# Values of the last head group computed as features by tokens, its eight units mixed two to a bank, and the first two tiles of the output projection taken half by half

## The chip, the cores and the metric

The kernel runs on one NeuronCore of one Trainium2 chip. The metric is the device time of one execution in microseconds (us), as a median over runs. The names of the engines are those of the profile: PE is TensorE, DVE is VectorE, ACT is ScalarE, POOL is GpSimd, SP is the engine that issues most of the transfers. PE has two clock levels, 1.2 and 2.4 GHz; the profile gives the granted one as a share of the higher.

## The reference

A decoder trunk of two layers over 1,024 tokens of width 1,024, all in float32. Cut to what matters here, one layer is:

```python
hn = rmsnorm(h, norm1[i])
z = hn @ w_in[i]                       # 256 pool columns, then q, k, v of 768 columns each
u = z[..., :POOL_WIDTH]
q, k, v = jnp.split(z[..., POOL_WIDTH:], 3, axis=-1)
...                                    # partial rotary on q and k; 12 heads of 64
pool_out = pool_mixer(u, pool_w[i], pool_scale[i])
attn_out = dilated_mixer(q, k, v)      # 3 head groups ("patterns") of 4 heads, each with its own
                                       # window and dilation; weighted by their softmax denominators
h = h + jnp.concatenate([pool_out, attn_out], axis=-1) @ w_out[i]
hn = rmsnorm(h, norm2[i])
h = h + jnp.square(jax.nn.relu(hn @ w_up[i])) @ w_down[i]
gate = jax.nn.sigmoid(rmsnorm(h, norm3[i]) @ w_gate[i])
h = h + gate * (p[i] @ w_ple[i])
```

The change lies at the end of the input projection (the 256 v columns of the third pattern), in that pattern's product of probabilities and values, and in the first two of eight column tiles of `w_out`.

## The kernel before, in words

Activations lie transposed: a tile holds 128 features by 1,024 tokens. Each is kept as a pair of fp32r tiles, high part and low part (`h`, `l`), and so is each weight (`wh`, `wl`), so that one product is three matmuls per 128 rows of the contraction: `wh` by `h`, `wh` by `l`, `wl` by `h`. `products` issues the 8 x 3 matmuls of 512 columns for one weight tile of 128 columns and one half (512) of the tokens.

The input projection goes in this order: q, k, v of pattern 0, of pattern 1, q and k of pattern 2, the two pool tiles `u0` and `u1`, and last v of pattern 2. The attention of a pattern is eight units of 128 queries. A unit takes four steps: `scores` on PE, `softmax` on DVE and ACT, `turn` (PE transposes of the probabilities into a bank tagged "e", and a copy to `et`), and `mix` (PE products of `et` with the values into a bank tagged "o", evacuated by `out`). These steps are strewn between the matmuls of the projection.

What decides that order is a clock in the program that builds the kernel, `Clock`. Every matmul of a product moves it on by an estimate (`tick`), and work that was put down for later (`at`, `go` with a delay, a `yield` in a generator) is issued when the clock passes its time. `need` and `until` are different: if something is not yet issued, they move the clock to the next pending piece of work and issue it, again and again, until it is, without a matmul in between. The order so found is fixed on each engine's queue; on the chip an instruction that waits holds up all that stands behind it on its engine.

The weights come through `Weights.next`: it needs the asked tile's high and low parts issued (`ck.need`), and starts the tile after it (`begin`), one of eight row blocks every 900 ns of that clock.

In the stage that is changed the other engines have this to do:

- the pool mixer: `mix_sums(1)` on POOL builds window sums `pa`, `pb` of `u1`; `mix_out` on DVE makes `py` from them; two matmuls `pm` on PE (one for each half) into "e" banks, evacuated to `cat0` and `cat1` by ACT (high part) and DVE (low part)
- `joint`: the weights of the three patterns, by small DVE operations, one PE transpose `jt` into an "e" bank, the DVE copy `jw`, and transfers through DRAM (`wt_d`) into tiles `wb` that are broadcast over the partitions
- `weigh`: DVE multiplies a pattern's output `o` by `wb`, ACT and DVE split it into the pair `cat2` to `cat7`, which the output projection reads.

There are 8 PSUM banks: three tagged "mm", two "s", two "e" and one "o". An "e" bank is given on when the copies out of it are done. The core of the code that is replaced, with `v2` as tokens by features:

```python
        for t in range(8):
            p = bank(f"v2p{L}", "mm", (128, 256))
            ...
                nc.tensor.matmul(p, h[:, tc_], wh, start=kk == 0, stop=False)
```

There the activations are the stationary operand and the weights the moving one, 256 columns, so no transpose of v is needed. Each unit's `mix` follows by itself once its 128 tokens are there.

Of the kernel before, what the change touches and what calls it, by code (L numbers as in the profile page):

```python
# [9 lines left out]
F32 = mybir.dt.float32  # L10
# [107 lines left out]
def body(nc, tc, pools, A, out):  # L118
# [3 lines left out]
    def blk(name, dt=F32, shape=(128, 1024)):  # L122
        return sb.tile(list(shape), dt, name=name, tag="b")

    def bank(name, tag, shape=(128, 512)):
        return ps.tile(list(shape), F32, name=name, tag=tag)
# [4 lines left out]
    def hs(hf):  # L131
        return slice(hf * 512, hf * 512 + 512)
# [207 lines left out]
    for L in range(DEPTH):  # L340
        wi, wo, wu, wd, wg = (A[n][L] for n in ("w_in", "w_out", "w_up", "w_down", "w_gate"))
        g1 = G_N1 + 8 * L

        def col(part, g):
            return POOLW + 768 * part + 256 * g

        for g in range(NPAT):
            for part in range(2 if g == 2 else 3):
                for m in range(2):
                    groups.append([(wi, 0, 8, col(part, g) + 128 * m, 128, g1)])  # L350
        for m in range(2):
            groups.append([(wi, 0, 8, 128 * m, 128, g1)])
        groups.append([(wi, 4 * a, 4, col(2, 2), 256, g1) for a in range(2)])
        for m in range(8):
            groups.append([(wo, 0, 8, 128 * m, 128, None)])
        sevens.append(([(wu, 0, 4, 256 * j) for j in range(FF // 256)],
                       [(wd, a, n, 256 * t) for t, a, n in STEPS]))
        dn0.append(len(groups))
        for rep in range(2 if L == DEPTH - 1 else 1):
            for m in range(8):  # L360
                groups.append([(wg, 0, 8, m * 128, 128, None)])
            for m in range(2):
                pgroups.append([(A["w_ple"][L], 0, 2, m * 512, 512, None)])
# [177 lines left out]
    def pair(name):  # L541
        return blk(name + "H", F32R), blk(name + "L", F32R)

    def products(p, w, rhs, cols, first=True, last=True):
        n = len(w)
        ns = 0.42 * (cols.stop - cols.start)
        for i in range(n):
            (wh, wl), (h, l) = w[i], rhs[i]
            ck.need((id(h), cols.start // 512))
            nc.tensor.matmul(p, wh, h[:, cols], start=first and i == 0, stop=False)  # L550
            ck.tick(ns)
            nc.tensor.matmul(p, wh, l[:, cols], start=False, stop=False)  # L552
            ck.tick(ns)
            nc.tensor.matmul(p, wl, h[:, cols], start=False, stop=last and i == n - 1)  # L554
            if i + 1 < n:
                ck.tick(ns)
        ck.now += ns
# [65 lines left out]
    def layer(L, hT, norm, tabs):  # L623
# [96 lines left out]
        oT = {}  # L720
        vdone = set()

        def vok(g, n, p):
            return ((2, n) if g == 2 else (g, p, n // 4)) in vdone

        def in_v(g):
            vs = []
# [127 lines left out]
        def attend(g, q, k, vget, base, gap, late):  # L855

            o = [blk(f"o{g}{p}_{L}") for p in range(2)]
            oT[g] = o
            units = [Unit(g, n, q, k, vget, o) for n in range(8)]

            def alone(u):
                yield 1500.0
                while not vok(g, u.n, 0):
                    yield 500.0
                u.mix()

            def beats():
                t = ck.now
                for i in range(8 + 2 * late):
                    if 0 <= i - late < 8:  # L870
                        u = units[i - late]
                        u.turn()
                        if g == 2:
                            ck.go(alone(u))
                    if g < 2 and i >= 2 * late:
                        u = units[i - 2 * late]
                        while not (vok(g, u.n, 0) and vok(g, u.n, 1)):
                            yield 500.0
                        u.mix()
                    if i < 8:  # L880
                        units[i].scores()
                    t += gap
                    yield max(100.0, t - ck.now)
            ck.go(beats(), delay=base)

        for g in range(2):
            q = in_qk(f"q{g}", g)
# [3 lines left out]
                   5000.0, 5900.0, 1)  # L891
        q = in_qk("q2", 2)
        k = in_qk("k2", 2)
        v2 = [blk(f"v2{a}_{L}", F32, (128, 4, 256)) for a in range(2)]
        attend(2, q, k, lambda n, h: v2[n // 4][:, n % 4, 64 * h:64 * h + 64],
               3500.0, 2500.0, 2)


        us = [blk(f"u{m}_{L}") for m in range(2)]
# [118 lines left out]
        def weigh(g, p, hf):  # L1018
            i = 2 * g + p
            keys = {("wb", g, p)}  # L1020
            for n in range(4 * hf, 4 * hf + 4) if g == 2 else range(8):
                keys.add(("o", g, n, 1))
            while keys & ck.waiting:
                yield 300.0
            o = oT[g][p][:, hs(hf)]
            nc.vector.tensor_tensor(o, o, wbc[g, p][:, hs(hf)], op=OP.mult)
            used.append((g, p))
            if used.count((g, p)) == 2:
                del wbc[g, p]
            yield 800.0  # L1030
            yield from split(cat[2 + i], o, hf)
# [11 lines left out]
        for i in range(4):  # L1043
            cat[2 + i] = pair(f"cat{2 + i}_{L}")
            for hf in range(2):
                ck.go(weigh(i // 2, i % 2, hf), (id(cat[2 + i][0]), hf), W_0 + W_1 * (2 * i + hf))
        for t in range(8):
            p = bank(f"v2p{L}", "mm", (128, 256))
            tc_ = slice(t * 128, t * 128 + 128)
            for kk in range(8):  # L1050
                h, l = hT[kk]
                wh, wl = (x[:, kk % 4] for x in w[kk // 4])
                nc.tensor.matmul(p, h[:, tc_], wh, start=kk == 0, stop=False)
                nc.tensor.matmul(p, l[:, tc_], wh, start=False, stop=False)
                nc.tensor.matmul(p, h[:, tc_], wl, start=False, stop=kk == 7)
                if kk < 7:
                    ck.tick(330.0)
            nc.scalar.activation(v2[t // 4][:, t % 4], p, AF.Copy, scale=norm.rt[:, t:t + 1])
            ck.at(600.0, lambda t=t: vdone.add((2, t)))
            ck.tick(330.0)  # L1060
            if t in (3, 7):
                for i in (4, 5):
                    if t == 3:
                        cat[2 + i] = pair(f"cat{2 + i}_{L}")
                    hf = t // 7
                    ck.go(weigh(2, i % 2, hf), (id(cat[2 + i][0]), hf), 2500.0 + 900.0 * (i - 4))


        norm2 = Norm(f"b{L}")
# [95 lines left out]
        S7 = Seven(sevens[L][0], seq, f"u{L}", side=4)  # L1165

        catl = [cat[i] for i in range(8)]
        for m in range(6):
            w = W.next()
            if m == 5:  # L1170
                W.begin(W.i + 1, delay=5000.0)
            for hf in range(2):
                p = bank(f"po{L}", "mm")
                products(p, wk(w, range(8)), catl, hs(hf))
                ck.go(out_evac(p, m, hf))
# [413 lines left out]
```

## Time and profile before

| | |
|---|---|
| median of 3 runs | 2268.42 us (2268.37 to 2268.53) |
| the profiled execution, device time | 2269.02 us |
| its span from first to last instruction | 2267.2 us |
| PE busy | 2240.3 us (99%), 11088 matmuls |
| DVE busy | 1643.2 us (72%) |
| ACT busy | 1011.6 us (45%) |
| POOL busy | 313.9 us (14%) |
| granted PE clock, mean | 0.999 |
| chain that ended last | PE 91%, DVE 5%, DMA 1%, ACT 1%, POOL 1% |

A matmul's time in the profile runs from its start to its modelled end, and neighbours overlap; what a matmul costs is read from the distance between starts. In the chain the overlap is taken off already.

### The profile page before, as it was taken

How to read it: one execution, taken by the hardware profiler on the slowest of the kernel's cores; microseconds unless marked ns; L12 is line 12 of the kernel's file. 1: busy time of each engine (PE TensorE's matmuls, PEld its weight loads, DVE VectorE, ACT ScalarE, POOL GpSimd, SP SyncE). 2: the span in 40 equal slices, each digit the busy share in tenths (PEclk: the TensorE clock that was granted, in tenths of full speed). 3: DMA queues.
4: the chain of work that ended last, by engine and by line, in shares of the span. 5: the costliest groups of instructions: out<-in, count | busy, mean ns of one | idle time of the engine just before them, and what ended most of it. 6: DMA issues, size and time to landing. Idle time of an engine off the chain costs nothing.

```text
span 2267.2 us, 30544 instructions
## 1 busy us (share of the span) xinstructions
PE 2240.3 (99%) x11088; PEld 1849.0 (82%) x11088; DVE 1643.2 (72%) x3046; ACT 1011.6 (45%) x2147; POOL 313.9 (14%) x282
## 2 busy tenths in 40 slices
PE   8999999999999999999999999999999999999998
PEld 6887788888887888878887878888888878888888
DVE  6565757877778888796565567687777798888845
ACT  6244533533335434364324355444333453434645
POOL 5121135100000000022121122330000000000322
PEclk9999999999999999999999999999999999999999
DMA  6011133354448745431220122234445675546224
GB/s 186 19 48 20 39 94 112 124 167 150 150 143 271 239 135 171 149 112 47 61 62 19 39 49 61 81 112 153 153 154 160 209 247 175 162 140 181 69 62 134
DMA packets 296367, 275.63 MB, mean 122 GB/s; under 512 B 12476, under 2 KB 224056, under 8 KB 296216
## 3 DMA queue, kind: packets, MB, share of 16 engines
q1 hardware_dynamic: 293624, 270.04, 38.6%
q0 software_dynamic: 2272, 3.61, 0.9%
q8 instruction: 87, 1.43, 0.3%
q14 instruction: 64, 0.52, 0.1%
q10 hardware_dynamic: 320, 0.03, 0.0%
HBM read 200.99 MB, written 72.58 MB: 121 GB/s over the span
## 4 chain that ended last, share of the span: by engine, by line
PE 91%; DVE 5%; DMA 1%; ACT 1%; issue 1%; POOL 1%; SPq 0%; DVEq 0%; ACTq 0%
PE X L567 29%; PE Z L567 14%; PE Y L567 7%; PE in L552 5%; PE in L554 5%; PE in L550 5%; PE gt L554 3%; PE gt L552 3%; PE gt L550 3%; PE po L552 2%; PE po L550 2%; PE po L578 2%; PE po L554 2%; PE o L836 2%; PE s L785 2%
## 5 line engine op out<-in xcount | busy, mean ns | idle before, releaser
L458 POOL TENSOR_TENSOR sq_c<-sq_c,sqt_c 128x512 f32<-128x512 f32 x28 | 41.8, 1496 | 1162.0 <-ACT sqt_c L456 1161.1
L567 PE MATMUL X<-wP,d0p 128*128 128x512 f32 x768 | 180.2, 390 | 3.2 <-DVE acc L1294 2.5
L567 PE MATMUL X<-wP,d1p 128*128 128x512 f32 x768 | 180.1, 390 | 3.2 <-DVE acc L1294 2.5
L567 PE MATMUL X<-xP,u1p 128*128 128x512 f32 x768 | 182.2, 389 | 0.0
L567 PE MATMUL X<-xP,u0p 128*128 128x512 f32 x768 | 182.2, 389 | 0.0
L567 PEld LDWEIGHTS X<-wP,d0p 128*128 128x128 f32 x768 | 143.8, 188 | 34.6 <-ACT wP L1275 2.0
L567 PEld LDWEIGHTS X<-wP,d1p 128*128 128x128 f32 x768 | 143.8, 188 | 34.6 <-ACT wP L1275 2.0
L1277 DVE TENSOR_TENSOR wP<-wP 128x512 fp32r<-128x512 f32 x252 | 171.0, 697 | 0.9 <-ACT wP L1275 0.9
L567 PEld LDWEIGHTS X<-xP,u1p 128*128 128x128 f32 x768 | 143.9, 188 | 29.8
L567 PEld LDWEIGHTS X<-xP,u0p 128*128 128x128 f32 x768 | 143.9, 188 | 29.8
L1235 ACT ACTIVATE y<-y 128x1024 f32<-128x1024 f32 x64 | 67.3, 1055 | 199.2 <-DVE y L1232 199.1
L191 DVE SCALAR_TENSOR_TENSOR wl<-wr,gt,wh 128x128 fp32r<-128x128 f32 (+1 forms) x288 | 117.8, 440 | 44.4 <-ACT wh L197 44.1
L1275 ACT ACTIVATE wP<-wP 128x512 fp32r<-128x512 f32 x252 | 146.7, 617 | 0.2
L1294 DVE TENSOR_TENSOR acc<-acc,X 128x512 f32<-128x512 f32 x128 | 87.4, 683 | 55.6 <-PE X L567 55.6
L804 ACT ACTIVATE sm<-sm,nm 128x128 f32<-128x128 f32 (+1 forms) x192 | 84.3, 440 | 79.9 <-DVE nm L801 77.6
L197 ACT ACTIVATE wh<-wr,gt 128x128 fp32r<-128x128 f32 (+1 forms) x304 | 101.8, 397 | 0.9 <-DMA wr<-in_w_in_dram 0.8
L680 POOL TENSOR_TENSOR rot<-rot,s 128x512 f32<-128x512 f32 x48 | 61.6, 1288 | 255.6 <-DVE rot L678 136.7
L567 PE MATMUL Z<-wP,d1p 128*128 128x512 f32 x384 | 92.1, 389 | 1.0 <-DVE acc L1294 1.0
L567 PE MATMUL Z<-wP,d0p 128*128 128x512 f32 x384 | 92.1, 389 | 1.0 <-DVE acc L1294 1.0
L567 PE MATMUL Z<-xP,u1p 128*128 128x512 f32 x384 | 91.6, 389 | 0.0
L567 PE MATMUL Z<-xP,u0p 128*128 128x512 f32 x384 | 91.6, 389 | 0.0
L567 PEld LDWEIGHTS Z<-wP,d0p 128*128 128x128 f32 x384 | 72.0, 188 | 16.4 <-DVE acc L1294 1.4
(474 smaller groups left out, 5510.1 us busy)
## 6 DMA issues: line engine op xcount, KB each, us to landing
wP<-x_d SPq DMA_DIRECT2D x252, 256.0 KB, 3.4
x_d<-ys SPq DMA_DIRECT2D x64, 512.0 KB, 3.7
wr<-in_w_in_dram SPq DMA_DIRECT2D x40, 512.0 KB, 4.2
u0r<-in_w_up_dram SPq DMA_DIRECT2D x32, 512.0 KB, 5.1
x_d<-y SPq DMA_DIRECT2D x32, 512.0 KB, 2.8
u1r<-in_w_up_dram SPq DMA_DIRECT2D x32, 512.0 KB, 5.4
d0r<-in_w_down_dram SPq DMA_DIRECT2D x28, 512.0 KB, 6.2
d1r<-in_w_down_dram SPq DMA_DIRECT2D x28, 512.0 KB, 5.9
```

What stands on the lines that cost most here:

```text
L191: nc.vector.scalar_tensor_tensor(l[:, k], raw[:, k], gs[k], f(h[:, k]), op0=OP.mult, op1=OP.subtract)
L197: nc.scalar.activation(h[:, k], raw[:, k], AF.Copy, scale=gs[k])
L550: nc.tensor.matmul(p, wh, h[:, cols], start=first and i == 0, stop=False)
L552: nc.tensor.matmul(p, wh, l[:, cols], start=False, stop=False)
L554: nc.tensor.matmul(p, wl, h[:, cols], start=False, stop=last and i == n - 1)
L567: nc.tensor.matmul(p, w[:, a, i], x[:, b], start=first and i == 0 and a == b == 0, stop=i == n - 1 and a == 1, skip_group_check=not first)
L680: nc.gpsimd.tensor_tensor(a, a, tb["s"][:, hs(hf)], op=OP.mult)
L804: nc.scalar.activation(self.sm[:, p, hh], self.sm[:, p, hh], AF.Exp, bias=nm[:, h:h + 1], scale=0.125, accum_out=ml[g][:, n, 4 + h:5 + h])
L1235: nc.scalar.activation(y, y, AF.Square)
L1275: nc.scalar.activation(t[:, 0], f(t[:, 1]), AF.Copy)
L1277: nc.vector.tensor_tensor(t[:, 1], f(t[:, 1]), f(t[:, 0]), op=OP.subtract)
L1294: nc.vector.tensor_tensor(a, a, p, op=OP.add)
```

## The change

The version before computes v of pattern 2 as tokens by features with 192 matmuls of 256 columns. The version after computes it like every other v, as features by tokens, with 96 matmuls of 512 columns from two weight tiles that are both held (`ws`), half by half: both tiles for tokens 0 to 511, then both for 512 to 1023. Four DVE evacuations with the norm's scale go to `vts`. For each half `mix_half` transposes the two tiles on PE (eight transposes, through "e" banks), copies them on ACT to `v2`, and then issues the four units of the half together, two to a bank, one bank tagged "o" and one "s", with four ACT copies of 256 columns. The first two tiles of the output projection are also both taken before their products, and done as tile 0 and tile 1 for the first half, then for the second.

```diff
-        groups.append([(wi, 4 * a, 4, col(2, 2), 256, g1) for a in range(2)])
+        for m in range(2):
+            groups.append([(wi, 0, 8, col(2, 2) + 128 * m, 128, g1)])
...
-            def alone(u):
-                yield 1500.0
-                while not vok(g, u.n, 0):
-                    yield 500.0
-                u.mix()
...
-                        if g == 2:
-                            ck.go(alone(u))
...
-        for t in range(8):
-            p = bank(f"v2p{L}", "mm", (128, 256))
...
+        ws = [w, W.next()]
+        vts = []
+        for m in range(2):
+            vts.append(blk(f"vt2{m}_{L}"))
+            v2.append(blk(f"v2{m}_{L}", F32, (128, 8, 128)))
+
+        def mix_half(b):
+
+            yield 2200.0
+            for m in range(2):
+                p = bank(f"vp2_{L}", "e", (128, 4, 128))
+                for i in range(4):
+                    n = 4 * b + i
+                    nc.tensor.transpose(p[:, i], vts[m][:, n * 128:n * 128 + 128], ident)
+                ck.now += 430.0
+                nc.scalar.activation(v2[m][:, 4 * b:4 * b + 4], p, AF.Copy)
+            yield 2000.0
+            for c in range(2):
+                us_ = units2[4 * b + 2 * c:4 * b + 2 * c + 2]
+                op = bank(f"o2_{L}", "os"[c], (128, 2, 2, 128))
...
+        for hf in range(2):
+            for m in range(2):
+                p = bank(f"in{L}", "mm")
+                products(p, wk(ws[m], range(8)), hT, hs(hf))
+                nc.vector.tensor_tensor(vts[m][:, hs(hf)], p, norm.bc[:, hs(hf)], op=OP.mult)
+            ck.go(mix_half(hf))
...
-        for m in range(6):
+        w = W.next()
+        ws = [w, W.next()]
+        for hf in range(2):
+            for m in range(2):
+                p = bank(f"po{L}", "mm")
+                products(p, wk(ws[m], range(8)), catl, hs(hf))
+                ck.go(out_evac(p, m, hf))
+        ws = None
+        for m in range(2, 6):
```

The second `W.next()` of the v stage stands directly behind the first. At that point the second tile's eight row blocks are not issued yet, so `need` moves the builder's clock on until they are, and other work that was put down for that time is issued too. Three places show it; `_0` in a name is the layer, the last number tells buffers apart.

On PE, where the second pool tile's last product (`in_2646`, or `in_2640`) ends and the v stage begins. Before:

```order
L554 MATMUL in_2646<-h_7H,wl_2338 128x512
L1053 MATMUL v2p_2750<-wh_2501,h_0H 128x256
L1054 MATMUL v2p_2750<-wh_2501,h_0L 128x256
L1055 MATMUL v2p_2750<-wl_2502,h_0H 128x256
L944 MATMUL pm_2754<-py_2636,pw_135 128x512
L1053 MATMUL v2p_2750<-wh_2501,h_1H 128x256
```

After:

```order
L555 MATMUL in_2640<-h_7H,wl_2334 128x512
L938 MATMUL pm_2744<-py_2630,pw_135 128x512
L938 MATMUL pm_2751<-py_2630,pw_135 128x512
L976 MATMUL jt_2765<-cst,jt 96x128
L551 MATMUL in_2781<-h_0H,wh_2497 128x512
L553 MATMUL in_2781<-h_0L,wh_2497 128x512
```

Both `pm` of the first pool tile and the transpose `jt` now stand ahead of the stage; before, the second `pm` stood after 18 and `jt` after 42 of its 192 matmuls.

On PE, around the second pool tile's two `pm`. Before, they stand in the sixth and seventh of eight token tiles:

```order
L1055 MATMUL v2p_2953<-wl_2504,h_6H 128x256
L944 MATMUL pm_2993<-py_2892,pw_135 128x512
L1053 MATMUL v2p_2953<-wh_2503,h_7H 128x256
...
L836 MATMUL o_3015<-et_2625,v_0_2327 64x128 x4
L944 MATMUL pm_3022<-py_2892,pw_135 128x512
L1053 MATMUL v2p_3004<-wh_2501,h_3H 128x256
```

After (`in_2872` is the third of the four v products, `vp` are the banks of the first half's transposes, `vt` the evacuated tiles):

```order
L555 MATMUL in_2872<-h_0H,wl_2498 128x512
L938 MATMUL pm_2878<-py_2813,pw_135 128x512
L551 MATMUL in_2872<-h_1H,wh_2497 128x512
L553 MATMUL in_2872<-h_1L,wh_2497 128x512
L555 MATMUL in_2872<-h_1H,wl_2498 128x512
L551 MATMUL in_2872<-h_2H,wh_2497 128x512
L1054 MATMUL vp_0_2890<-cst,vt_0_2777 128x128 x4
L1054 MATMUL vp_0_2896<-cst,vt_0_2779 128x128 x4
L938 MATMUL pm_2905<-py_2813,pw_135 128x512
L553 MATMUL in_2872<-h_2L,wh_2497 128x512
```

The first of them now stands 51 matmuls of 512 columns into the stage, and the second seven places behind, after the transposes. In this version `vp_0_2896` and then `pm_2905` get the "e" bank of `vp_0_2890`, one after the other, each after ACT's copy out of it.

On DVE, between the evacuation of `u1` and that of the first half's second v tile (`vt_0_2779`), after the change:

```order
L988 TENSOR_TENSOR u_0_2329<-in_2640,rs_a_484 128x512
L191 SCALAR_TENSOR_TENSOR wl_2735<-wr_2495,gt,wh_2734 128x128
L539 SCALAR_TENSOR_TENSOR cat_0L<-pm_2744,gt,cat_0H 128x512
L191 SCALAR_TENSOR_TENSOR wl_2735<-wr_2495,gt,wh_2734 128x128 x2
...
L181 TENSOR_TENSOR wl_2776<-wr_2732,wh_2775 128x1024
L925 SCALAR_TENSOR_TENSOR py_2813<-pa_2717,cst,u_0_2329 64x1024
...
L535 TENSOR_TENSOR cat_0L<-o_0_879,cat_0H 128x512
L1077 TENSOR_TENSOR vt_0_2779<-in_2820,rs_a_484 128x512
L1020 TENSOR_TENSOR o_0_1703<-o_0_1703,wb 128x512 x2
L535 TENSOR_TENSOR cat_0L<-o_0_1703,cat_0H 128x512 x2
```

New behind `u` are the eight `wl` of the second v tile (before, a tile of 256 columns was all made ahead of `u`), and the two `vt` evacuations stand behind `py` and behind four multiplications and four splits of `weigh`. ACT's copy out of `vp_0_2890` stands behind both splits of `o_0_1703` and behind that of `pm_2878`.

## Rows read from the trace of the kernel before

**Rows 1.** Waits of PE over the span: total us, times, longest.

```profile
PE o L836 <- ACT v L1058: 0.6, 2, 0.3
```

**Rows 2.** Windows of the changed stage in layer 0 and layer 1.

```profile
281.46:313.87 32.41, 32.13 (x259) 28.01 (x258) 22.79 (x42) 14.26 (x35) 11.88 (x11) 1.00 0.46 116
1393.40:1425.80 32.40, 32.12 (x259) 28.00 (x258) 22.72 (x42) 14.23 (x35) 11.89 (x11) 1.00 0.46 116
```

**Rows 3.** Timeline of PE, layer 0: start us, us, instruction.

```profile
282.78 0.28 PE L1054 MATMUL v2p<-wh,h_1L 128*128 128x256 f32 x1
...
284.34 0.28 PE L1055 MATMUL v2p<-wl,h_5H 128*128 128x256 f32 x1
...
313.71 0.40 PE L550 MATMUL po<-cat_0H,wh 128*128 128x512 f32 x1
```

**Rows 4.** The chain that ended last: start us, us, what; overlap taken off.

```profile
248.99 1.07 PE o L836 x16
...
257.97 0.44 PE e L817 x4
...
281.97 0.86 PE pm L944 x2
...
286.90 0.59 PE o L836 x8
287.49 0.32 PE v2p L1053
...
380.00 21.76 PE po L578 x96
```

**Rows 5.** Timeline of DVE in the stage, layer 0.

```profile
282.89 0.68 DVE L994 TENSOR_TENSOR u<-in,rs_a 128x512 f32<-128x512 f32 x1
283.49 1.21 DVE L181 TENSOR_TENSOR wl<-wr,wh 128x1024 fp32r<-128x1024 f32 x1
...
289.26 0.29 DVE L985 COPY jw<-jt 96x128 f32<-96x128 f32 x1 [1.20 <-PE jt L982]
292.70 3.00 DVE L931 SCALAR_TENSOR_TENSOR py<-pa,cst,u 64x1024 f32<-64x1024 f32 x1 [3.16 <-POOL pa L911]
...
296.01 1.28 DVE L931 SCALAR_TENSOR_TENSOR py<-pb,cst,u 64x1024 f32<-64x1024 f32 x1
...
297.62 2.54 DVE L1026 TENSOR_TENSOR o<-o,wb 128x512 f32<-128x512 f32 x4
```

**Rows 6.** Timeline of POOL in the stage, layer 0.

```profile
283.65 3.01 POOL L905 TENSOR_TENSOR pa<-u 128x896 f32<-128x896 f32 x1 [34.03 <-DVE u L994]
...
287.29 1.84 POOL L905 TENSOR_TENSOR pb<-pa 128x768 f32<-128x768 f32 x1
...
292.48 0.19 POOL L911 COPY pa<-pb 128x4 f32<-128x4 f32 x1
292.75 1.88 POOL L910 TENSOR_TENSOR pb<-pa 64x1016 f32<-64x1016 f32 x1
294.57 1.20 POOL L911 COPY pb<-pa 64x8 f32<-64x8 f32 x1
```

**Rows 7.** Instructions of line L191: ns min/median/max, first and last start.

```profile
L191 DVE SCALAR_TENSOR_TENSOR wl<-wr,gt,wh x288: 334/345/1264, 30.6 to 1391.6; 128x128 fp32r<-128x128 f32 x136, 128x256 fp32r<-128x256 f32 x8
```

**Rows 8.** Timeline of ACT in the stage, layer 0.

```profile
279.29 0.57 ACT L827 ACTIVATE et<-e 128x512 f32<-128x512 f32 x1
...
306.56 0.68 ACT L536 ACTIVATE cat_0H<-pm,gt 128x512 fp32r<-128x512 f32 x1
...
309.06 0.62 ACT L532 ACTIVATE cat_0H<-o 128x512 fp32r<-128x512 f32 x1
```

**Rows 9.** Timeline of PE at the kernel's start, and a window behind its last matmul.

```profile
7.49 3.03 PE L605 MATMUL xp<-cst,x 128*128 128x128 f32 x13 [0.72 <-DMA x<-in_x_dram]
...
12.82 0.60 PE L605 MATMUL xp<-cst,x 128*128 128x128 f32 x4
...
2262.00:2264.00 2.00, 0.00 (x0) 0.00 (x0) 0.70 (x2) 0.61 (x1) 0.00 (x0) 0.50 0.57 214
```

More of the change, by code (lines that the diff above doesn't have):

```diff
@@ L723, in vok @@
         def vok(g, n, p):
-            return ((2, n) if g == 2 else (g, p, n // 4)) in vdone
+            return (g, p, n // 4) in vdone
         def in_v(g):
@@ L884, in attend @@
             ck.go(beats(), delay=base)
+            return units
         for g in range(2):
@@ L893, in layer @@
         k = in_qk("k2", 2)
-        v2 = [blk(f"v2{a}_{L}", F32, (128, 4, 256)) for a in range(2)]
-        attend(2, q, k, lambda n, h: v2[n // 4][:, n % 4, 64 * h:64 * h + 64],
-               3500.0, 2500.0, 2)
+        v2 = []
+        units2 = attend(2, q, k, lambda n, h: v2[h // 2][:, n, 64 * (h % 2):64 * (h % 2) + 64],
+                        3500.0, 2500.0, 2)
         us = [blk(f"u{m}_{L}") for m in range(2)]
@@ L1046, in layer @@
                 ck.go(weigh(i // 2, i % 2, hf), (id(cat[2 + i][0]), hf), W_0 + W_1 * (2 * i + hf))
-        for t in range(8):
-            p = bank(f"v2p{L}", "mm", (128, 256))
[L1049 to L1066, printed above, removed]
+        ws = [w, W.next()]
@@ new lines, in layer @@
+        vts = []
[15 more added lines that the diff above has]
+                op = bank(f"o2_{L}", "os"[c], (128, 2, 2, 128))
+                for i, u in enumerate(us_):
+                    for p, hh, h in u.heads:
+                        nc.tensor.matmul(op[64 * hh:64 * hh + 64, i, p], u.vget(u.n, h), u.et[:, p, hh, 0],
+                                         start=True, stop=True)
+                ck.now += 860.0
+                n = us_[0].n
+                for p in range(2):
+                    nc.scalar.activation(oT[2][p][:, n * 128:n * 128 + 256]
+                                         .rearrange("p (i c) -> p i c", i=2), op[:, :, p], AF.Copy)
+                for u in us_:
+                    ck.waiting.discard(("o", 2, u.n, 1))
@@ new lines, in layer @@
+        for hf in range(2):
[4 more added lines that the diff above has]
+            ck.go(mix_half(hf))
+            for i in (4, 5):
+                if hf == 0:
+                    cat[2 + i] = pair(f"cat{2 + i}_{L}")
+                ck.go(weigh(2, i % 2, hf), (id(cat[2 + i][0]), hf), 6500.0 + 900.0 * (i - 4))
@@ L1167, in layer @@
         catl = [cat[i] for i in range(8)]
-        for m in range(6):
+        w = W.next()
[5 more added lines that the diff above has]
+                ck.go(out_evac(p, m, hf))
+        ws = None
+        for m in range(2, 6):
             w = W.next()
```

## The prediction, made before the changed kernel ran

> **What bounds the kernel now.** I looked first at the shares of busy time: PE works 2240.3 of 2267.2 us, so the span is PE's queue and nothing else, unless PE waits. Then at PE's waits: in the stage that is changed it waits for 0.3 us in each layer, for ACT's copy of a v tile [rows 1]. The windows of the stage say the same: 32.4 us, of which PE is busy 32.1, with 259 matmuls in each layer [rows 2]. The two layers are alike, so I work out layer 0 and count it twice. The stage runs from 281.46, the first matmul of v [rows 2], to 313.71, the first of the output projection [rows 3]. Two things can change the time: how many microseconds of work PE gets, and whether an instruction in its queue now stands there before its input is ready. The second needs the timelines of DVE, POOL and ACT, which have slack now that nobody pays for.
>
> **PE's work, per layer.** The prices are distances between starts. A 256-column matmul costs (284.34 - 282.78) / 13 = 0.12 us [rows 3]. A 512-column one costs 21.76 / 96 = 0.227 [rows 4]. A transpose costs 0.44 / 4 = 0.11, a `pm` 0.86. A unit's eight `o` passes cost 0.59, and the v matmul behind them 0.32 where 0.12 is usual, so 0.79 in all; sixteen passes cost 1.07, so eight more in one go cost 0.48 [rows 4].
>
> - Before: the measured 32.25 from 281.46 to 313.71, with seven of the units in it, and the eighth, 0.79, inside the output projection: 33.04.
> - After: 96 x 0.227 = 21.76; four `pm` 3.44; 16 transposes 1.76; `jt` 0.1; two groups of four units, each 0.79 + 3 x 0.48 = 2.23: together 31.5.
>
> So the work alone saves 1.5 us in a layer, 3.0 in both. The halved number of weight loads gives nothing of its own; the matmul pitches have it in them. The reordering of the first two output tiles moves no work and costs nothing: the same four products follow each other, and the second half's `cat6` and `cat7` are asked for one product (5.4 us) later than before.
>
> **PE's waits.** I walk the new order with the old durations.
>
> *First wait, `jt`.* PE ends `u1` at 281.46 and does two `pm` until 283.2. Behind them stands `jt`, which needs the "e" bank of the first `pm`. DVE frees that bank after `u` (next start 283.49 [rows 5]), one `wl` (0.345 [rows 7]) and a `cat_0L` of some 0.7. That gives 284.5, a wait of 1.2. All v products are queued behind it. Two of them and three matmuls later, 0.1 + 10.9 + 0.7, PE is at the second tile's `pm` at 296.2.
>
> *Second wait, `pm_2878`.* It needs `py`, which DVE makes from POOL's `pa`. Before, POOL began at 283.65 and its last `pa` ended at 292.67 [rows 6], and `py` was waited for by nobody; now PE asks at 296.2. DVE is no longer free meanwhile: eight `wl` and the 1.21 us `wl` of the output weights stand ahead of `py`. These read two SBUF operands each, and the rows show what happens when POOL works: `py` takes 3.00 beside POOL's 1.88 and 1.28 without [rows 5, 6], POOL's tiny copy takes 1.20 instead of 0.19 when it comes second [rows 6], and one `wl` took 1.264 against a median of 0.345 [rows 7]. One of the two engines stands still, and the one that waited goes next. So I add them: POOL's 9.0, less the 0.9 that its first operation (3.01; by the second's rate 896 / 768 x 1.84 = 2.15) waited for DVE, is 8.2; eight `wl` 2.8; the large `wl` 1.2; POOL's 1.88; `py` 1.28. From 283.5 that ends at 298.9. Then come the small corrections of `py` twice (0.7), `vt` (0.7 like `u`) and the second `py`, 1.28: 301.5. PE waits 5.3 us.
>
> The Trainium skill (SBUF — State Buffer, "shared port pair" under Terms) states this as an exclusive lock between VectorE and GpSimd, held for a whole instruction, for VectorE operations with two SBUF inputs too; by it the sum above is a queue, and by the row before alone, without new blocking, `py` would end 3.2 us earlier.
>
> *Third wait, `vp_0_2896`.* It needs ACT's copy out of `vp_0_2890` to free the bank, and ACT has that copy behind the splits of `o_0_1703`. DVE from 301.5: four multiplications 2.5 [rows 5], four splits 2.5, `vt` 0.7, two multiplications 1.3: 308.5. ACT: one split 0.62, `cat_0H` from `pm` 0.68, the copy 0.57 [rows 8]: 310.4. PE has done `pm`, four matmuls and four transposes since 301.5 and stands from 303.7: 6.7 us. Then four transposes, another ACT copy (0.57, as `pm_2905` needs the same bank), and `pm`: 312.4.
>
> The `wb` tiles come no later than that: `jw` moves from 289.26 to about 291.1 (six `wl` and POOL's 5.5 after 283.5), and 8.4 us behind `jw` the multiplications found them [rows 5], so 299.5 against 301.5.
>
> *Last wait.* From 312.4 PE has 17 matmuls, a group of units and the fourth product, 3.9 + 2.2 + 5.4: 323.9. The second half's transposes need the last `vt` on DVE, behind a `cat_0L` that is held until then: 0.7 + 0.7, then four transposes 0.44. The output projection begins at 325.8.
>
> Sum per layer: 325.8 + 2.23 for the units that now lie in the projection, against 313.71 + 0.79: 13.5 us longer. All later work hangs on PE and moves with it; there is hardly a wait behind it to give time back.
>
> **The clock.** PE now stands idle for over 5 us twice, with 2.2 us of work between. Where it came out of idleness at the kernel's start, 13 transposes took 3.03, 0.23 each against 0.11: half pace, though the granted clock shows nothing there; at 12.82 four took 0.60, their usual time with the last one's tail [rows 9]. Behind the last matmul the granted clock is 0.50, the lower level [rows 9]. No row shows PE come back from an idle stretch in the middle. The bounds are nothing, if the clock stays up, and 2.7, half of the stretch from 7.49 to 12.82; the 13 transposes alone lost 3.03 - 13 x 0.11 = 1.6. I take 2 per layer, since the start's rows are the nearest. The Trainium skill (TensorE: Matmul & The Clock Gate, "HAM oscillation — how this bites in real kernels") says that waits between groups of matmuls put PE back to the half clock; by it the loss comes in both layers, and no run yet shows it here.
>
> **Sum.** 2269.02 + 2 x (13.5 + 2) = 2300.0 for the profiled execution, which lay 0.6 above the median: 2299.4, say 2299.
>
> **Rivals.**
>
> - *The clock stays up.* Then 2269.0 + 27.0 - 0.6 = 2295.4. For it: only an end and a start show otherwise. Against it: 0.50 behind the last matmul.
> - *POOL and DVE don't hold each other up further.* The `wl` end early, `py` starts at 292.7 as before, everything is 3.2 us earlier per layer: 2289, or 2293 with the clock's loss. Against it: rows 6 and 7.
> - *Longer.* A 512 KB weight load now stands ahead of the `wb` transfers in SP's queue, and DVE may lose more turns to POOL: 3 to 6 us more per layer, 2305 to 2311.
> - *Not slower: the waits are covered.* If `py` and the bank's copy were ready when PE comes, only the saved work counts: 2268.4 - 3.0 = 2265.4, no difference that a measurement of this kernel can tell (some 0.2%, 4.5 us). For that PE's arrival at `vp_0_2896`, without waits at about 297, must find ACT's copy done, which the sum puts at 310. It decides from there: every microsecond of the 13 that is wrong comes off.
>
> **How the numbers follow.** Forecast (2296 to 2304, with the clock's loss) 0.45; clock up 0.15; no further blocking 0.2; longer 0.12; something between 2275 and 2288 0.03; not slower 0.05. The range is 2284 to 2311. Faster by over 0.2% 0.01, within 0.2% 0.05, slower 0.94.
>
> **What would show it.** In the new profile PE's waits should name `vp` behind ACT's `v` and `pm` behind DVE's `py`, some 7 and 5 us in each layer; the window from 281.46 to the first `po` should be about 44 to 47 us instead of 32.3 with some 30 of PE work; the granted clock in it should fall behind the second long wait. `py` should start near 297, not 292.7, and the copy into `v` near 310. It is wrong if PE's in-order queue is not held by those waits, if `weigh` runs earlier than the `wb` rows allow me to see, or if the extra idle time is given back behind the output projection.

## The result, and the profile after

The changed kernel takes 2293.15 us (median of 4 runs, 2293.0 to 2293.4) against 2268.39 for the kernel before (4 runs): 24.8 us longer, ratio 1.0109, 95% interval 1.0094 to 1.0124. The profiled execution's span is 2291.2 us against 2267.2, so 24.0 more.

The view of PE's waits, the one to read first: engine and line, what it waited for, total us, times, longest. Before, the changed stage had 0.6 us of waits in it [rows 1]; now it has these:

```profile
PE vp L1054 <- ACT v L1056: 10.7, 2, 6.2
...
PE pm L938 <- DVE py L933: 4.4, 2, 2.2
...
PE vp L1054 <- DVE vt L1077: 1.6, 2, 0.8
PE pm L938 <- ACT v L1056: 1.4, 2, 0.7
...
PE jt L976 <- DVE cat_1L L539: 1.0, 1, 1.0
PE jt L976 <- DVE cat_0L L539: 1.0, 1, 1.0
```

All five waits that the prediction walks through are there, in both layers, with the releasers that it names; together 20.1 us. Where they lie is seen in PE's timeline of layer 0 (start, us, instruction; in brackets the idle time before it and what ended it):

```profile
280.50 1.88 PE L938 MATMUL pm<-py,pw 128*128 128x512 f32 x4
283.37 0.31 PE L976 MATMUL jt<-cst,jt 128*96 128x128 f32 x1 [0.99 <-DVE cat_0L L539]
...
297.47 1.13 PE L938 MATMUL pm<-py,pw 128*128 128x512 f32 x2 [2.18 <-DVE py L933]
...
299.35 0.60 PE L1054 MATMUL vp<-cst,vt 128*128 128x128 f32 x4
306.18 1.12 PE L1054 MATMUL vp<-cst,vt 128*128 128x128 f32 x4 [6.24 <-ACT v L1056]
307.99 2.07 PE L938 MATMUL pm<-py,pw 128*128 128x512 f32 x2 [0.69 <-ACT v L1056]
...
310.28 0.63 PE L555 MATMUL in<-h_2H,wl 128*128 128x512 f32 x1
...
312.55 2.11 PE L1063 MATMUL o<-et,v 128*64 128x128 f32 x32
...
324.07 0.66 PE L1054 MATMUL vp<-cst,vt 128*128 128x128 f32 x4 [0.79 <-DVE vt L1077]
324.48 0.47 PE L551 MATMUL po<-cat_0H,wh 128*128 128x512 f32 x1
```

The stage lasts from 280.50 to 324.48, 43.98 us, where it took 32.25 before ([rows 2, 3]). Between 306.18 and 312.55 the same instructions take nearly twice their usual time: four transposes 1.12 for 0.60, a matmul 0.63 for 0.40. The windows say why (us, then busy us and instructions of PE, PEld, DVE, ACT, POOL, then the granted clock, DMA share, GB/s):

```profile
280.50:324.48 43.98, 33.09 (x154) 24.15 (x153) 32.58 (x54) 14.91 (x30) 12.21 (x11) 0.88 0.34 87
...
299.00:304.00 5.00, 0.94 (x7) 0.57 (x5) 5.00 (x9) 1.94 (x4) 0.00 (x0) 0.86 0.77 199
304.00:314.00 10.00, 7.13 (x36) 4.66 (x38) 4.20 (x7) 4.01 (x8) 0.00 (x0) 0.56 0.01 2
...
308.00:310.00 2.00, 2.00 (x3) 0.97 (x4) 0.00 (x0) 0.00 (x0) 0.00 (x0) 0.50 0.00 0
```

From within the long wait to about 313 PE is given the lower of its two levels, 1.2 GHz (0.50).

Who made PE wait: the timeline of DVE.

```profile
288.31 0.28 DVE L979 COPY jw<-jt 96x128 f32<-96x128 f32 x1
288.51 2.46 DVE L191 SCALAR_TENSOR_TENSOR wl<-wr,gt,wh 128x128 fp32r<-128x128 f32 x2
290.89 1.21 DVE L181 TENSOR_TENSOR wl<-wr,wh 128x1024 fp32r<-128x1024 f32 x1
292.03 2.90 DVE L925 SCALAR_TENSOR_TENSOR py<-pa,cst,u 64x1024 f32<-64x1024 f32 x1
...
295.83 1.28 DVE L925 SCALAR_TENSOR_TENSOR py<-pb,cst,u 64x1024 f32<-64x1024 f32 x1
...
298.30 1.89 DVE L1020 TENSOR_TENSOR o<-o,wb 128x512 f32<-128x512 f32 x3 [0.16 <-DMA wb<-wt_d]
...
302.52 0.68 DVE L1077 TENSOR_TENSOR vt<-in,rs_a 128x512 f32<-128x512 f32 x1
303.12 1.28 DVE L1020 TENSOR_TENSOR o<-o,wb 128x512 f32<-128x512 f32 x2
```

Then ACT's, where the copy into `v` stands behind two splits of `o` and one of `pm`, as in the order that the front part shows; and POOL's first and last steps:

```profile
303.83 1.23 ACT L533 ACTIVATE cat_0H<-o 128x512 fp32r<-128x512 f32 x2 [2.98 <-DVE o L1020]
304.97 0.67 ACT L537 ACTIVATE cat_0H<-pm,gt 128x512 fp32r<-128x512 f32 x1
305.54 0.59 ACT L1056 ACTIVATE v<-vp 128x512 f32<-128x512 f32 x1
```

```profile
282.54 2.11 POOL L899 TENSOR_TENSOR pa<-u 128x896 f32<-128x896 f32 x1 [33.37 <-DVE u L988]
...
290.77 0.26 POOL L905 COPY pa<-pb 128x4 f32<-128x4 f32 x1
291.10 2.75 POOL L904 TENSOR_TENSOR pb<-pa 64x1016 f32<-64x1016 f32 x1
```

Two things were not foreseen. `py` is done at 297.4 and not at 301.5. And the stage begins earlier than before, by more than the 0.44 us by which this execution is ahead since the kernel's first matmuls. PE's timeline ahead of the stage, first of the kernel before, then of the changed one:

```profile
278.65 1.12 PE L817 MATMUL e<-cst,sm 128*128 128x128 f32 x4
279.53 0.48 PE L552 MATMUL in<-h_5L,wh 128*128 128x512 f32 x1
```

```profile
278.21 0.60 PE L818 MATMUL e<-cst,sm 128*128 128x128 f32 x4
278.56 0.48 PE L553 MATMUL in<-h_5L,wh 128*128 128x512 f32 x1
```

The transposes of the eighth unit held PE 0.88 us before and 0.35 now: 0.53 us less, the same in layer 1. They wait inside their group for ACT's exponential of the unit, which DVE's row maxima release; on DVE `wl` blocks of 256 columns (0.48 us each) stood between that unit's operations, now blocks of 128 (0.35). That the smaller blocks bring it is read from the timelines; no run tried it alone.

From these transposes in layer 0 to the same in layer 1 it is 1402.71 - 278.21 = 1124.50 us against 1390.56 - 278.65 = 1111.91 before, 12.6 more; from there to the end 888.5 against 876.6, 11.9 more. Nothing is given back later: from the projection's first matmul to the next layer's stage it is 1405.00 - 324.48 = 1080.5 against 1079.7, and the 0.8 is, to within 0.3, the four units that now lie there (1.90 for 0.79) less the 0.53.

### The profile page after: what moved, and what is told of

It reads as the page before. It is cut to its first block, busy times and chain, and to the rows that moved or that the text cites. A ratio compares the mean times of both kernels' runs of the same rounds, so it can differ in the third digit from the quotient of the medians.

```text
span 2291.2 us, 30248 instructions
## 1 busy us (share of the span) xinstructions
PE 2244.8 (98%) x10928; PEld 1845.4 (81%) x10928; DVE 1662.1 (73%) x3070; ACT 1011.3 (44%) x2139; POOL 312.9 (14%) x282
## 4 chain that ended last, share of the span: by engine, by line
PE 89%; DVE 6%; issue 1%; ACT 1%; DMA 1%; POOL 0%; SPq 0%; DVEq 0%; ACTq 0%
PE X L568 28%; PE Z L568 14%; PE Y L568 6%; PE in L553 6%; PE in L555 6%; PE in L551 5%; PE gt L555 3%; PE gt L553 3%; PE gt L551 3%; PE po L553 2%; PE po L555 2%; PE po L551 2%; PE po L579 2%; PE s L786 2%; PE o L837 1%
## 5 line engine op out<-in xcount | busy, mean ns | idle before, releaser
L191 DVE SCALAR_TENSOR_TENSOR wl<-wr,gt,wh 128x128 fp32r<-128x128 f32 x304 | 131.6, 465 | 44.4 <-ACT wh L197 44.0
L197 ACT ACTIVATE wh<-wr,gt 128x128 fp32r<-128x128 f32 x320 | 105.4, 392 | 0.5 <-DMA wr<-in_w_in_dram 0.5
L568 PEld LDWEIGHTS Z<-wP,d1p 128*128 128x128 f32 x384 | 72.0, 188 | 16.4 <-DVE acc L1319 1.4
```

The lines of the kernel that those rows point to most:

```text
L191: nc.vector.scalar_tensor_tensor(l[:, k], raw[:, k], gs[k], f(h[:, k]), op0=OP.mult, op1=OP.subtract)
L197: nc.scalar.activation(h[:, k], raw[:, k], AF.Copy, scale=gs[k])
L568: nc.tensor.matmul(p, w[:, a, i], x[:, b], start=first and i == 0 and a == b == 0, stop=i == n - 1 and a == 1, skip_group_check=not first)
```

## Experiments

Each run is set against runs of the kernel before that were measured beside it, whose medians were 2268.3 to 2268.6; the changed kernel stands at 2293.15.

**Is it the order?** The second v tile is asked for only ahead of its first product, so that the builder's clock doesn't jump.

```diff
-        w = W.next()
+        w = W.next(prefetch=False)
+        W.load_to(W.i + 2)
+        W.begin(W.i, 500.0, 600.0)
...
-        ws = [w, W.next()]
+        ws = [w]
...
+                if len(ws) <= m:
+                    ws.append(W.next())
```

> The changed kernel, except that the second weight tile of the v stage is asked for only ahead of its first product, and its eight row blocks are put down every 500 ns of the builder's clock, so that nothing makes that clock jump; stage, banks, transposes and output projection stay. Theory A (the loss is the order that the jump leaves in the queues: waits for py and for ACT's copy of v, and the low clock behind them): no wait of PE over 1 us in the stage, clock 1.00 there, and what is left is the saved work, 1.5 us a layer, with the 0.5 us a layer that the eighth unit's softmax comes earlier: about 2264.5 us (2262 to 2268), 28 to 29 us below the changed kernel. Theory B (the new stage itself costs it: transposes, bank sharing, eight small wl beside POOL): above 2280.

Measured: 2274.34 us, ratio 1.0026 (1.0016 to 1.0037). The waits for `py`, for ACT's copy and for `jt` are gone, so theory B falls; but the time is 10 us over my number and outside its range, since another wait came up at the stage's end, with the low clock behind it (waits of PE, then a window):

```profile
PE vp L1056 <- DVE vt L1081: 6.0, 2, 3.0
```

```profile
313.00:318.00 5.00, 5.00 (x14) 3.71 (x14) 3.14 (x4) 3.39 (x5) 0.00 (x0) 0.50 0.34 96
```

**The jump left in, the timers moved past it.**

```diff
-T_M1, W_0, W_1 = 13000.0, 9000.0, 1800.0
+T_M1, W_0, W_1 = 21000.0, 17000.0, 1800.0
```

> The changed kernel, with the second weight tile still asked for at once (the builder's clock still jumps by some 8 us), but the two timers for the second pool tile's pm and for the weighing of patterns 0 and 1 set 8 us later, T_M1 21000 and W_0 17000. Theory A (only the order counts): the waits for py and for ACT's copy of v are gone, the wait of 1.0 us ahead of jt stays in each layer: about 2266.5 us (2264 to 2270). Theory B (the stage itself costs it): above 2280. A rival within A: the later weighing makes the output projection wait for cat4 to cat7: 2272 to 2280, with the wait named there.

Measured: 2269.68 us, ratio 1.0007 (0.9998 to 1.0016), in the range and 3 us over its middle: besides `jt`'s 1.0 in each layer a wait for the second half's `vt` is left:

```profile
PE vp L1054 <- DVE vt L1077: 2.6, 2, 1.6
```

The stage's transposes, banks and grouped units are all in this run; 23.5 of the 24.8 us are gone by two timers of the builder's clock. `W_0` is the timer of `weigh` and of the transfers that fetch the `wb` tiles, so both move.

**One timer alone, that of `weigh`** (`W_0` 17000, `T_M1` as it was). The other one alone was not tried.

> The changed kernel with one timer 8 us later, that of the weighing of patterns 0 and 1 (W_0 17000); the builder's clock still jumps and the second pool tile's pm stays where it is. Then two of the six splits, and no longer all six, stand ahead of the copy of v on ACT. Theory A (PE's longest wait is ACT's queue order): the wait for py stays at 2.2 us, ACT's copy starts at about 301.3 in place of 305.5, PE's wait for it shrinks from 6.2 to some 1.7 us; 4.5 us a layer, and 2.7 more if the clock then stays up: 2279 to 2284 us. Rival (what ACT's copy waits for comes down the chain of POOL, py and DVE, whatever the order of the splits): 2291 to 2293.

Measured: 2279.83 us, ratio 1.0049 (1.0036 to 1.0062). The wait for `py` stays (4.4 us over both layers, as in the changed kernel) and ACT's copy comes 5.3 us earlier; PE waits 1.2 us for it in layer 0. ACT's timeline, then DVE's second `vt` of the first half:

```profile
298.55 1.23 ACT L533 ACTIVATE cat_0H<-o 128x512 fp32r<-128x512 f32 x2 [12.96 <-DVE o L1020]
299.69 0.67 ACT L537 ACTIVATE cat_0H<-pm,gt 128x512 fp32r<-128x512 f32 x1
300.26 0.58 ACT L1056 ACTIVATE v<-vp 128x512 f32<-128x512 f32 x1
```

```profile
297.23 0.69 DVE L1077 TENSOR_TENSOR vt<-in,rs_a 128x512 f32<-128x512 f32 x1
```

So PE's longest wait hangs on the place of the `weigh` work in the queues, and the rival falls: 13.3 us go with this timer. That it is the place in ACT's queue alone is not shown, since the timer takes the work out of DVE's queue too: the second `vt`, which the same transposes need, comes at 297.23 in place of 302.52.

**Is it the bank?** The first half's transposes go to the "s" banks.

```diff
-                p = bank(f"vp2_{L}", "e", (128, 4, 128))
+                p = bank(f"vp2_{L}", "e" if b else "s", (128, 4, 128))
```

> The changed kernel with the first half's two groups of transposes in the two s banks, free by then, in place of the e banks; nothing else changes. Then the second group waits only for DVE's vt (303.2), and pm for nothing. Theory A (the wait of 6.2 us is for the bank, and the units need the copies only seven matmuls later): the units start at about 306.7 in place of 312.5, 5.8 us earlier a layer; 2281.5 us if the clock stays up, up to 2286 if the wait for vt drops it. Rival (the copy itself is what PE needs, whatever the bank): the wait moves to the units, 2290 to 2293.

Measured: 2284.01 us, ratio 1.0068 (1.0054 to 1.0082), between theory A's two numbers. The units start at 306.95. The wait for the copy is gone and one for DVE's `vt`, which had been covered by it, is seen in its place, 3.1 us in layer 0 and 3.3 in layer 1, with a clock of 0.63 in the mean of the 4 us behind the first:

```profile
302.46 1.09 PE L1054 MATMUL vp<-cst,vt 128*128 128x128 f32 x4 [3.11 <-DVE vt L1077]
```

The bank makes the copy's lateness cost some 4.6 us a layer. In the changed kernel that `vt` was done at 303.20, so of the wait from 299.94 to 306.18 only the last 3 us are the copy's by itself; DVE's queue would have made the first 3.3 as well.

**Do POOL and DVE hold each other up?** The window sums of the second pool tile are left out.

```diff
-                for _ in mix_sums(1):
-                    pass
+                sums[1] = us[1], us[1]
```

> The changed kernel without POOL's window sums of the second pool tile (py is made from u1 itself; this part of the computation is left out), so that the eight wl, the weights' large wl and py meet no POOL work. Theory A (DVE stands still for POOL's operations and the waits are ends of one DVE queue): each wl takes 0.35 us, py is ready at about 291, the wait for it is gone, jw and with it the wb tiles come 2.7 us earlier, and so does the copy of v; PE's wait for it grows to 7 or 8 us but ends 2.8 us earlier: 2293 - 5.5 = 2287.5 us (2286 to 2290). If POOL holds up nothing that PE waits for: 2293. If the two waits are independent (only the 2.2 us for py go): 2288.7, with the v copy at the same time as before.

Measured: 2287.07 us, ratio 1.0081 (1.0067 to 1.0095), the time that theory A gives. The wait for `py` is gone, `jw` comes 3.1 us earlier and the copy of v 3.4 us (302.13 for 305.54), so the two waits are not independent. One part of theory A failed: PE's wait for the copy did not grow, it shrank from 6.24 to 5.28 us in layer 0. The eight `wl` of one layer, by groups (count, busy us, mean ns, idle before), in the changed kernel and without POOL's work:

```profile
L191 DVE SCALAR_TENSOR_TENSOR wl<-wr,gt,wh 128x128 fp32r<-128x128 f32 x8 | 7.4, 959 | 0.0
```

```profile
L191 DVE SCALAR_TENSOR_TENSOR wl<-wr,gt,wh 128x128 fp32r<-128x128 f32 x8 | 2.4, 344 | 0.0
```

DVE loses 5.0 us on them and 1.6 on the first `py` (2.90 against 1.27). POOL loses little to the short `wl`: from its first start to the end of the last `pa` it took 8.5 us in the changed kernel (282.54 to 291.03), where the prediction had reckoned 8.2 for POOL alone, and its copy 0.26 for 0.19 [rows 6]. To the large `wl` of 1.21, which came first, it does lose: the operation that began at 291.10 took 2.75, against 1.88 [rows 6]. The Trainium skill (SBUF — State Buffer, "shared port pair" under Terms) has the pair as an exclusive lock held for a whole instruction, the loser blocked; 959 ns beside POOL and 344 without agree for DVE; that POOL lost next to nothing to the short `wl` is what the runs add.

**The clock.** 24 matmuls that nobody reads fill the longest wait, between the first half's two groups of transposes.

```diff
+                if b == 0 and m == 1:
+                    pf = bank(f"fill{L}", "mm")
+                    for k in range(24):
+                        nc.tensor.matmul(pf, ws[0][0][0][:, k % 8], hT[k % 8][0][:, :512], start=k == 0, stop=k == 23)
```

> The changed kernel with 24 matmuls of 512 columns more in each layer, between the first half's two groups of transposes; their result is read by nobody. They lie in PE's longest wait (6.2 and 4.5 us; 24 x 0.227 = 5.4) and keep PE busy there. Theory A (behind that wait PE runs at half clock for some 7 us, and that is 3 to 4 us a layer of its own): granted clock 1.00 behind the wait, the waits for ACT's copies end as before, 2285 to 2288 us. Theory D (the clock costs nothing, or falls whether PE is busy or not): 2293 or above, up to 2296 in the layer where the matmuls are longer than the wait.

Measured: 2288.68 us, ratio 1.0090 (1.0073 to 1.0107): 4.5 us less, with more work on PE, 0.7 above theory A's range and well under theory D's. Layer 0, two windows and PE's timeline:

```profile
299.00:304.00 5.00, 5.00 (x26) 4.13 (x25) 5.00 (x9) 1.97 (x4) 0.00 (x0) 1.00 0.71 192
304.00:314.00 10.00, 8.57 (x60) 6.19 (x59) 5.61 (x10) 5.65 (x12) 0.00 (x0) 1.00 0.05 20
```

```profile
306.15 0.66 PE L1058 MATMUL vp<-cst,vt 128*128 128x128 f32 x4 [0.75 <-ACT v L1060]
307.49 1.13 PE L938 MATMUL pm<-py,pw 128*128 128x512 f32 x2 [0.69 <-ACT v L1060]
```

The transposes are released at the same 306.2, and with the clock at 1.00 the units start at 309.93 in place of 312.55: the low clock costs 2.6 us in layer 0. In layer 1 the filling is longer than the wait (4.5) and delays the transposes by 0.8, so less is left there. The Trainium skill (TensorE: Matmul & The Clock Gate, "HAM oscillation — how this bites in real kernels") says that waits between groups of matmuls put PE back to half clock; the changed kernel and this run show it for the wait of 6.2 us.

**The projection's order**, undone alone in the changed kernel, and undone in a kernel without the waits:

```diff
-        w = W.next()
-        ws = [w, W.next()]
-        for hf in range(2):
-            for m in range(2):
...
-        for m in range(2, 6):
+        for m in range(6):
```

> The changed kernel with the first two tiles of the output projection taken one after the other, as in the kernel before; only that part is undone. Theory A (this part moves no work and costs nothing): 2293 us, within 1.5. Theory C (it buys or costs something): if the second half's cat6 and cat7, asked 5.4 us earlier in this order, come too late, 2296 to 2300; if holding both weight tiles delays a load, 2288 to 2291.

Measured: 2291.98 us, ratio 1.0104 (1.0089 to 1.0119), within theory A's 1.5 us; the intervals of this run and the changed kernel overlap. It isn't quite the same, though: its four runs (2291.05 to 2292.73) lie below all four of the changed kernel, and the wait of 0.8 us a layer for the second half's `vt` is not there, since the projection's second `W.next()` is undone with the order.

> As the run beside it (both weight tiles asked for late), but with the first two tiles of the projection one after the other as in the kernel before: only the order of the first four projection products differs. If the order of the products is worth nothing by itself: within 1 us of that run, about 2264. If taking both first halves first covers a late cat6 or cat7 of the second half: 1 to 4 us more, 2265 to 2268.

Measured: 2266.75 us, ratio 0.9993 (0.9985 to 1.0002); its pair with the projection half by half (next run) 2266.57. The order of the four products is worth nothing.

**Removing what is left.** In the run of the first experiment the wait for `vt` was there since the projection's own second `W.next()` made the clock jump too and put the second half's transposes ahead of it. Asked for late as well:

```diff
-        ws = [w, W.next()]
+        ws = [w]
...
+                if len(ws) <= m:
+                    ws.append(W.next())
                 p = bank(f"po{L}", "mm")
```

> As the run with the second v tile asked for late (every 500 ns a row block), and the second tile of the output projection asked for only ahead of its first product too, so that the second half's transposes fall some ten matmuls into the projection instead of ahead of it. Theory A (only the order counts; the run before kept a wait of 3.0 us for the second half's vt in each layer, with some low clock behind it): no wait over 0.5 us is left in the stage; work saved 1.7 us and the earlier softmax 0.5 us in each layer: 2268.5 - 4.4 = 2264 us (2262 to 2267). Rival: the wait for vt only moves, cat6 and cat7 come late to the projection: 2266 to 2272 with that wait named.

Measured: 2266.57 us, ratio 0.9993 (0.9984 to 1.0002); a wait for `vt` of 1.3 us in layer 0 and 0.6 in layer 1 stays. Moving those transposes still later (3500 for 2200 in `mix_half` of the second half):

> As e5_lazy_both, with the second half's transposes put down 3500 ns of the builder's clock behind the last v product in place of 2200, so that they stand 16 and not 10 matmuls inside the projection. e5 kept a wait of 1.3 us for the second half's vt in layer 0 (1.9 over both layers). Theory A: that wait goes, 2265 us (2264 to 2266.5), 1 to 2 us below e5. Rival: cat7 of the first half, now asked for 0.9 us behind those transposes, or cat6 and cat7 of the second half, made later by as much, become the wait: 2266 to 2270.

Measured: 2271.10 us (12 runs: one of 4913.99, which nothing here explains, the others 2269.68 to 2272.89), ratio 1.0011 (1.0002 to 1.0020), 1 us above the rival's range. The rival's wait is the one that came: `cat7` of the first half is late in both layers. In layer 0 the clock falls behind that, though PE stood for less than 2 us; in layer 1 it stays at 1.00 behind the longer wait (waits of PE, then a window of layer 0):

```profile
PE po L551 <- ACT cat_1H L533: 1.9, 1, 1.9
PE po L551 <- ACT cat_0H L533: 1.6, 1, 1.6
```

```profile
318.00:320.00 2.00, 2.00 (x10) 1.25 (x10) 0.69 (x1) 0.00 (x0) 0.94 (x1) 0.50 0.08 24
```

So the other end: what makes DVE late there is the first `wb` tile, which comes 9.6 us behind `jw` (DVE in e5_lazy_both):

```profile
300.37 2.50 DVE L1020 TENSOR_TENSOR o<-o,wb 128x512 f32<-128x512 f32 x4 [3.28 <-DMA wb<-wt_d]
```

`jt` is put earlier, by the delay ahead of it in `joint` (7000; 5200 and 4000 in two runs).

> As e5_lazy_both, with the transpose jt of the pattern weights put down 5200 ns of the builder's clock behind its inputs in place of 7000: it stands eight matmuls earlier in PE's queue and jw two wl earlier in DVE's. In e5 DVE stood still for 3.3 us until the first wb tile came, 9.6 us behind jw, and the second half's vt, which PE waits for, stands behind that work. Theory A: jw and wb come about 1.8 us earlier, the wait for vt of 1.3 us in layer 0 and 0.6 in layer 1 goes: 2264.5 us (2263.5 to 2266), 2 us below e5. Rival: vt waits for something else (the split behind pm), or jw stands still for POOL all the same: 2266 to 2267, as e5.

Measured: 2265.78 us, ratio 0.9988 (0.9979 to 0.9997). The wait for `vt` is gone, but the second pool tile's `py` now stands on DVE behind the multiplications that wait for `wb`, and PE stands ahead of its `pm`, 1.7 us in layer 0 and 1.0 in layer 1. The profile names no engine for these two; that they are for `py` is read from the times (`py` done at 303.08, `pm` at 303.18 in layer 0, 1414.01 and 1414.12 in layer 1).

> As the run beside it with 4000 ns: jt stands 14 matmuls earlier than in e5, jw behind the third wl. Theory A: the same 2264.5 us, as no wait for vt is left to save beyond the first 1.8 us (2263.5 to 2266). Rival: jt now waits in PE's queue for the bank that DVE's cat_0L gives free, some 0.5 us a layer: 2265.5 to 2267.

Measured: 2264.17 us (11 runs, 2263.96 to 2264.74), ratio 0.9981 (0.9973 to 0.9990): 4.3 us below the kernel before, 29.0 below the changed one. Its list of PE's waits has none in the stage, in either layer; in layer 0 PE is busy for 31.87 us of 31.87, at a clock of 1.00:

```profile
280.63:312.50 31.87, 31.87 (x166) 25.01 (x165) 29.85 (x51) 14.73 (x30) 11.24 (x11) 1.00 0.54 134
```

## Why the prediction was right, and where a term was mis-sized

The mechanism held: the stage's work is less, PE stands for inputs that the builder's clock took for ready, and the clock falls behind the longest wait. The forecast was 2299, the measurement 2293.15, inside the range, but below the 2296 to 2304 that were held most likely. Two of the signs named ahead were missed: `py` started at 292.03 and not near 297, and the copy into `v` at 305.54 and not near 310.

- **Work, -1.5 us a layer.** Right. The run without waits is 4.3 us below the kernel before: 2 x 1.5, and 2 x 0.53 for the eighth unit's softmax, make 4.1. The rival "not slower" had its price right too, 2265.4; its condition, inputs ready when PE comes, needed three edits.
- **`jt`, 1.2.** 0.99 and 1.00.
- **`pm` for `py`, 5.3: the mis-sized term.** It measured 2.18 and 2.21. The step that failed is "So I add them". The sum of POOL's and DVE's operations let each delay the other. In fact DVE paid almost alone: by the starts in the two timelines a `wl` lasted until the running POOL operation ended (the second one from 283.23 to 284.79, POOL's first operation from 282.54 to 284.65), and POOL's chain ran nearly as it does by itself. Counted from POOL's start the first `py` ended after 12.4 us (282.54 to 294.93), where the sum has 15.4 (283.5 to 298.9); the 3.0 between them is about the eight `wl`, 2.8. With -3.1 us in each layer this is most of the miss. The rival "POOL and DVE don't hold each other up further" had the right start for `py` (292.7; measured 292.03) and, with the clock's loss, the right time, 2293. Its reason was wrong: the `wl` did not end early, they took 7.4 us for 2.4. They fitted into the time that `py` had to wait for POOL's `pa` anyway, so its hit is in part luck.
- **`vp` for ACT's copy, 6.7.** 6.24 in layer 0, with the releaser named. The copy ran at 305.5 and not near 310, but PE came earlier as well, at 299.9 and not at 303.7; both follow from the 4 us that `py` was earlier. Behind it `pm` waited 0.69, as reckoned. In layer 1 the wait is 4.47: there the clock fell already behind the wait for `py`, and PE came later by the 1.7 us that it lost so, while the copy did not (PE, layer 1):

```profile
1421.99 1.89 PE L938 MATMUL pm<-py,pw 128*128 128x512 f32 x2 [2.21 <-DVE py L933]
...
1424.11 0.63 PE L553 MATMUL in<-h_1L,wh 128*128 128x512 f32 x1
...
1430.58 1.11 PE L1054 MATMUL vp<-cst,vt 128*128 128x128 f32 x4 [4.47 <-ACT v L1056]
```

- **The last wait, 1.** 0.79 in both layers.
- **The `wb` tiles** were said to come in time; they did so by a hair, 0.16 us of waiting for the second. In the later runs they are what DVE waits for.
- **The clock, 2 a layer.** 2.6 in layer 0, near the upper bound of 2.7, which was worked out from another stretch, so that it comes this close is luck. The filled waits gave back 4.5 over both layers, with the 0.8 that they cost in layer 1 taken off already. That PE's clock falls behind the second long wait was said, and the window shows 0.56 where it was 1.00.
- **The projection's order, nothing.** Right, by two pairs of runs. What did cost something there is the second `W.next()`, a second jump of the builder's clock; it put the transposes ahead of the projection, and with them the last wait: 0.8 us a layer here, and 7.8 us between the two runs that differ by it alone (2274.34 to 2266.57).

Layer 0 adds up so: waits 0.99 + 2.18 + 6.24 + 0.69 + 0.79 = 10.9, low clock 2.6, work and softmax -2.1, together 11.4 of the 12.6. A wait is counted from the modelled end of the matmul before it, and neighbours else overlap by some 0.17 (0.40 less the pitch of 0.23); five waits make 0.9 of the 1.2 that is left. Against the forecast of 15.5 a layer, 12.6 and 11.9 are the `py` term's 3.1 and the 0.5 of the softmax, with smaller ones of both signs.

## What to carry to other kernels

Where a program's own clock sets the order of in-order queues, a call that moves that clock without work behind it is a change to every queue: look for the timers that run out in the jump, and either move the call to where its result is used or move the timers by as much. A change that saves PE work in a stage is only worth its saving when the inputs on DVE and ACT are ready by the new arrival; price the wait that a bank or a queue place makes, and the half clock behind it, before the saving. In this kernel short DVE operations (0.34 us alone) beside a chain of longer POOL ones cost DVE the rest of the POOL operation that was running and POOL almost nothing, while a DVE operation of 1.21 us that came first did hold POOL up; for a case like the first, count POOL's chain as fixed and DVE's work as what slips.

## What the runs showed of the hardware that was not expected

The granted clock did not follow from the length of a wait alone. Behind the 2.2 us for `py` it stayed at full speed in layer 0 of the changed kernel (window 297 to 299: 1.00) and fell in layer 1, whose next matmuls took 0.63 for 0.40, in the same execution and at the same place of the program; in e2_projection_as_before it was the other way round (0.54 in layer 0 at 297 to 299, 1.00 in layer 1). In e9_second_half_later it fell in layer 0 behind 1.6 us with 0.2 more soon after, and stayed at 1.00 in layer 1 behind 1.9 with 0.2 more; behind 1.6 us in e4_timers_moved and 1.3 in e5_lazy_both it did not fall. In layer 1 of the changed kernel it was back at 1.00 from 1427 to 1429, while PE stood still, and at 0.51 in the two microseconds from 1429. What makes the difference stays open.

DVE's and POOL's losses to each other are not alike: eight short `wl` took 7.4 us for 2.4, and the chain of POOL that they met 8.5 for 8.2.
